# RWKV-7 recurrence: outputs made with features on partitions, products moved to the merges, and scores spread over the k stage

## The chip, the cores and the metric

The kernel runs on one core of one Trainium2 chip. The metric is the device time of one execution in microseconds (us); the median of three runs before the change is 2640.33 us (2639.37 to 2643.1). Five engines work beside each other, each in the order of its own program: TensorE (PE; its weight loads are PEld), VectorE (DVE), ScalarE (ACT), GpSimd (POOL) and SyncE (SP), which issues the DMAs.

## What is computed

A decoder trunk of two layers over 272 tokens (16 learned ones ahead of 256) with 2048 features: first an RWKV-7 time mix with an MLP behind it, then a gated linear attention with an MLP. The change touches only the time mix. Cut to what matters:

```python
r, k, v = xr @ w_rkv[0], xk @ w_rkv[1], xv @ w_rkv[2]      # 2048 x 2048 each
kk = kk / max(norm per head, 1e-12)                        # heads of 64 features
def step(S, inp):                                          # one token, S is 64 x 64 for each of 32 heads
    r_t, w_t, k_t, v_t, a_t, b_t = inp
    sa = einsum('bhvk,bhk->bhv', S, a_t)
    S = S * w_t + sa (x) b_t + v_t (x) k_t
    y = einsum('bhvk,bhk->bhv', S, r_t)
y = (y - mean) * rsqrt(var + eps) * ln_w + ln_b            # per head
out = ((y + bonus) * g) @ w_o                              # g: low-rank gate
```

The kernel doesn't run 272 steps. It takes chunks of 64 tokens, in which the recurrence becomes small matrix products and a triangular system.

## The kernel before, in words

Activations stand with features on partitions and tokens in the free dimension: 16 tiles of 128 features by 272 tokens. Every large product is split into two parts of float32: a weight tile of 128 x 1024 (`raw`) is rounded by ScalarE to `hi` (L134) and VectorE takes the rest, `lo` (L135); three products (L140 to L142) then make one 128 x 128 block of weights, which is called a unit below. `wload` puts these three steps ahead of other work by a priority; apart from the stretch named below a scheduler fixes the order on each engine by priorities and its own estimate of times.

**The k stage** is the loop over 16 output tiles f with L452. Each tile takes 16 units, then ScalarE and VectorE make decayed and normalised keys (`kk`, `kn`), with one product that sums over heads (L465) and one for the bonus (L480), and write the operands `bk` and `ar` to memory (`bkd`, `ard`). Output tiles lie in PSUM banks: `pj` (two) for even f, `pt` (two, from `ptr`) for odd f. For the recurrence, four groups g of eight heads (four feature tiles) are formed. In tile 3 the mixed input of the v projection is made, in tile 4 `load(0)` fetches the operands of group 0 (`BK`, `AR`), and in tile 6 all five calls of `scores(0, c)` follow each other: for each chunk eight products (L416) into two `pt` banks, and a mask by VectorE (L268, `AM`). From tile 8 on, seven steps per tile of `invert(0)` are added: VectorE inverts the triangular systems with transposes (L431, L434, L445, L449) and 30 pairs of small operations on `sysA`.

**The recurrence** comes after. In it the order on TensorE is the order of the code (`manual_schedule`); the other engines stay with the scheduler. `R(n)` runs n units of the products that wait to be done (the v projection, then the output product, in all 512 units), `until(n)` runs them up to the nth. For each group g and each of five chunks c (four of 64 tokens, one of 16) a step consists of `state` (L597, products with the state `sb`), `R(GAPS[g][c][0])`, `solve` (L607), `centre` (v minus its mean, every other chunk, L558), `carry` (L617, the old state times the identity into a new accumulator), `R(GAPS[g][c][1])`, `learn` (L623, the new state), `inner` for the next chunk (L579), `emit` (L632, the outputs, tokens on partitions, into the only bank `pry`) and `keys` (L569). ScalarE copies the output to `yc` (L635); one step later `turn` (L643) turns it by products with the identity to features on partitions, and ScalarE copies that to `hres` (L645). In between stand, for the next group, `scores(g + 1, c)` in the first two steps and the steps of `invert(g + 1)` from the end of step 1, nine at a time; for the last group, `norm` (L656 and L665 with what lies between them), two calls at a time in steps 2 and 3.

A group ends with `until(MARK[g])`, then `merge(g + 1)` joins the two halves of each inverse: one transpose (L526), a copy into `AMr` (L527), products L535, four copies, products L545, four copies. Then come `centre`, `keys` and `inner` of the new group's first chunk.

Of the kernel before, what the change touches and what calls it, by code (L numbers as in the profile page):

```python
# [45 lines left out]
GAPS = [[(2, 1), (2, 1), (8, 8), (9, 9), (9, 9)],  # L46
# [7 lines left out]
class Kern:  # L54
# [211 lines left out]
    def rwkv(self, done):  # L266
# [185 lines left out]
        for f in range(KT):  # L452
            r = rr[f]
            bk, ar = st2[0][f % 2], st2[1][f % 2]
            ps = self.proj(pair(wk, f), xk, T, bank=self.ptr if f % 2 else None)
# [27 lines left out]
            if f == 3:  # L483
                xv = mix(3, self.xp)
                early2.close()
                wl = ExitStack()
                lp = wl.enter_context(tc.tile_pool(name="wl", bufs=1, reuse_waits="tile"))
                BKs, ARs = ([self.t(lp, [P, 4, 576], n)] for n in ("BK0", "AR0"))
                AMs, AMrs = [self.t(lp, [P, NC4, 8, 128], "AM0")], [self.t(lp, [64, 8, 64], "AMr0")]
                sysA = self.t(lp, [P, 32, 32], "sysA")  # L490
                t11 = sysA.rearrange("p a b -> p (a b)")[64:96].rearrange("p (c h s) -> p c h s", c=NC4, h=8)
                nc.gpsimd.memset(sysA, 0.0)
            if f == 4:
                load(0)
# [17 lines left out]
        uvs, ras, bkts, rys, ys, pSs = {}, {}, {}, {}, {}, {}  # L512

        def geom(g, c):
            full = c < NC4
            n = C if full else 32
            lo, up = slice(0, n), slice(n, 2 * n)


            return full, n, C if full else T - NC4 * C, (AMs[g % 2][:, c] if full else AMrs[g % 2]), lo, up, ((lo, up), (up, lo))  # L520


        def merge(g):
# [3 lines left out]
            nc.scalar.copy(AMr[32:64, :, 0:16].rearrange("p h t -> p t h"), rg[:, :, 0:8])  # L527
# [46 lines left out]
        def inner(g, c):  # L574
            full, n, nr, am, lo, up, at = geom(g, c)
            uv = uvs[g, c]
            ra = ras[g, c] = half(self.pu())
            for h in range(8):
                nc.tensor.matmul(ra[at[h % 2][0], h // 2], am[:n, h, :n], uv[:n, h], start=h < 2, stop=c == 0 and h > 5)  # L579
            if c == 0:  # L580
                sides(g, c)

        def sides(g, c):
            full, n, nr, am, lo, up, at = geom(g, c)
            rs = ras[g, c, "rs"] = self.t(kp, [P, 512], "rs", 2).rearrange("p (h v) -> p h v", h=8)
            for q in range(2):
                nc.scalar.mul(rs[up, q::2], ras[g, c][at[q][0]], -1.0)


        def state(g, c):  # L590
# [3 lines left out]
            for p in range(4):  # L594
                for q, i in ((0, 0), (1, 1), (1, 0), (0, 1)):
                    rows = slice(64 * q, 64 * q + 64)
                    nc.tensor.matmul((ra, ry)[i][at[q][i], p], AR[rows, p, c * 128 + i * n : c * 128 + (i + 1) * n],  # L597
                                     sb[rows, p], start=i == 1 and p == 0, stop=i == 0 and p == 3)
# [14 lines left out]
        def carry(g, c):  # L613
            pS = pSs[g, c] = half(self.pu())
            if c:
                for p in range(4):
                    nc.tensor.matmul(pS[:, p], self.ident, sb[:, p], start=p == 0, stop=False)  # L617
# [9 lines left out]
        def emit(g, c):  # L627
# [7 lines left out]
            nc.scalar.copy(y[: 2 * n], ry[: 2 * n])  # L635

        def turn(g, c):
            full, n, nr = geom(g, c)[:3]
            y, py = ys[g, c], self.ptr()
            for p in range(4):  # L640
                for q in range(2):
                    rows = slice(n * (1 - q), n * (1 - q) + n)
                    nc.tensor.matmul(py[64 * q : 64 * q + 64, p * C : p * C + n], y[rows, p], self.ident[rows, rows],  # L643
                                     start=True, stop=True)
            nc.scalar.copy(hres[:, 4 * g : 4 * g + 4, c * C : c * C + nr],  # L645
                           py[:, : 4 * C].rearrange("p (f t) -> p f t", f=4)[:, :, :nr])

        def norm(g):
            for f in range(4 * g, 4 * g + 4):

                g2 = self.t(kp, [P, 2, P], "g2", 2)
                nc.sync.dma_start(g2, ap["g2"][f])
                sq = self.t(kp, [P, T], "ysq", 2)
                nc.scalar.activation(sq, hres[:, f], AF.Square)
# [3 lines left out]
                nc.scalar.activation(sq, sq, AF.Exp, scale=-0.5)  # L658
                yield
# [3 lines left out]
                pg = self.pm()[:, :T]  # L663
# [100 lines left out]
        with tc.manual_schedule(engines={mybir.EngineType.PE}):  # L764
# [4 lines left out]
            next(m)  # L769
            until(64)  # L770
            for f in (centre, keys, inner):
                f(0, 0)
            inv = last = nothing
            for g in range(NG):
                more = g + 1 < NG
                for c in range(5):
                    if c:
                        state(g, c)
                        turn(g, c - 1)
# [12 lines left out]
                    some(last, 2 if more and 1 < c < 4 else 0 if more else 4)  # L792
# [18 lines left out]
                if more:  # L811
# [11 lines left out]
                else:  # L823
                    turn(g, 4)
# [259 lines left out]
```

## Time and profile before

| | us |
|---|---|
| median of three runs | 2640.33 |
| profiled execution | 2640.85 |
| its span, first to last instruction | 2639.1 |
| k stage, first product of tile 0 to the first merge | about 165 to 332 |
| recurrence from the first merge to the last step | 332 to 640 |

The page of a profile gives busy times of each engine, the chain of work that ended last, and groups of instructions by line. Answers of the trace are shown in four forms. A row of a stage gives its bounds, its length, busy times of PE, PEld, DVE, ACT and POOL with counts, the granted TensorE clock (1 is full), and the share and rate of the DMA engines. A row of waits names who waited for whom: the sum in us, how often, and the longest. A row of the timeline has the start, the duration, the engine, the line and operation, what is written and read, and in brackets idle time ahead of it with what ended it. A product of two float32 operands stands twice in a count (x16 for eight products). Matmuls overlap, so what one costs is the distance from its start to the next start.

### The profile page before, as it was taken

How to read it: one execution, taken by the hardware profiler on the slowest of the kernel's cores; microseconds unless marked ns; L12 is line 12 of the kernel's file. 1: busy time of each engine (PE TensorE's matmuls, PEld its weight loads, DVE VectorE, ACT ScalarE, POOL GpSimd, SP SyncE). 2: the span in 40 equal slices, each digit the busy share in tenths (PEclk: the TensorE clock that was granted, in tenths of full speed). 3: DMA queues.
4: the chain of work that ended last, by engine and by line, in shares of the span. 5: the costliest groups of instructions: out<-in, count | busy, mean ns of one | idle time of the engine just before them, and what ended most of it. 6: DMA issues, size and time to landing. Idle time of an engine off the chain costs nothing.

```text
span 2639.1 us, 47851 instructions
## 1 busy us (share of the span) xinstructions
PE 2564.8 (97%) x19588; PEld 2373.6 (90%) x19588; DVE 1661.4 (63%) x2734; ACT 1271.9 (48%) x2075; POOL 10.8 (0%) x35
## 2 busy tenths in 40 slices
PE   7998998989999999999999999999999999999998
PEld 7887887878999999999999989998888888888887
DVE  8677966674755545545546666676766656656565
ACT  5364644455544434434434454454555535445444
POOL 0000000000000000000000000000000000000000
PEclk9998998999999999999999999999999999999999
DMA  5565742232455555545555544454555555555554
GB/s 195 175 216 204 242 148 81 96 103 93 162 176 176 176 176 176 176 176 176 176 176 176 182 147 151 145 176 144 189 186 188 187 190 186 191 185 190 188 188 160
DMA packets 137084, 450.18 MB, mean 171 GB/s; under 512 B 15760, under 2 KB 23696, under 8 KB 136864
## 3 DMA queue, kind: packets, MB, share of 16 engines
q1 hardware_dynamic: 136864, 447.12, 48.9%
q8 instruction: 153, 2.51, 0.4%
q14 instruction: 67, 0.55, 0.1%
HBM read 431.07 MB, written 15.99 MB: 169 GB/s over the span
## 4 chain that ended last, share of the span: by engine, by line
PE 90%; DVE 5%; ACT 2%; DMA 2%; issue 1%; SPq 0%; DVEq 0%; ACTq 0%
PE pj L168 23%; PE pj L140 15%; PE pj L142 15%; PE pj L141 15%; PE pj L169 12%; DVE lo L135 1%; PE pt L416 1%; PE pj L195 1%; ACT hi L134 1%; PE pt L919 1%; DVE sysA L431 0%; PE pm L665 0%; DVE upd L268 0%; PE pm L558 0%; DVE sysA L268 0%
## 5 line engine op out<-in xcount | busy, mean ns | idle before, releaser
L134 ACT CAST hi<-raw 128x1024 fp32r<-128x1024 f32 (+1 forms) x834 | 813.5, 983 | 1085.0 <-PE pj L141 565.0
L135 DVE TENSOR_TENSOR lo<-raw,hi 128x1024 fp32r<-128x1024 f32 (+1 forms) x834 | 946.9, 1142 | 607.1 <-ACT hi L134 598.2
L140 PE MATMUL pj<-x,hi 128*128 128x272 f32 x2224 | 657.3, 296 | 9.6 <-ACT x L308 4.3
L142 PE MATMUL pj<-x,lo 128*128 128x272 f32 x2224 | 646.3, 291 | 2.9 <-DVE lo L135 2.8
L141 PE MATMUL pj<-x,hi 128*128 128x272 f32 x2224 | 644.0, 290 | 0.0
L168 PE MATMUL pj<-x,hi 128*128 128x512 f32 x1664 | 587.1, 396 | 0.6 <-DVE x L838 0.6
L169 PE MATMUL pj<-x,lo 128*128 128x256 f32 x1664 | 467.4, 281 | 1.3 <-DVE lo L135 1.3
L140 PEld LDWEIGHTS pj<-x,hi 128*128 128x128 f32 x2224 | 421.6, 190 | 17.9 <-ACT x L308 5.0
L141 PEld LDWEIGHTS pj<-x,hi 128*128 128x128 f32 x2224 | 424.3, 191 | 2.1
L142 PEld LDWEIGHTS pj<-x,lo 128*128 128x128 f32 x2224 | 421.3, 189 | 4.7 <-DVE lo L135 3.7
L168 PEld LDWEIGHTS pj<-x,hi 128*128 128x128 f32 x1664 | 313.2, 188 | 76.9 <-issue 2.9
L168 PE MATMUL pj<-h,hi 128*128 128x512 f32 x1024 | 358.5, 394 | 0.0
L169 PEld LDWEIGHTS pj<-x,lo 128*128 128x128 f32 x1664 | 314.1, 189 | 2.3 <-DVE lo L135 1.9
L140 PE MATMUL pj<-h,hi 128*128 128x272 f32 x1024 | 294.7, 288 | 0.0
L142 PE MATMUL pj<-h,lo 128*128 128x272 f32 x1024 | 293.9, 287 | 0.0
L141 PE MATMUL pj<-h,hi 128*128 128x272 f32 x1024 | 293.6, 287 | 0.0
L169 PE MATMUL pj<-h,lo 128*128 128x256 f32 x1024 | 288.5, 282 | 0.0
L168 PEld LDWEIGHTS pj<-h,hi 128*128 128x128 f32 x1024 | 192.4, 188 | 44.5
L141 PEld LDWEIGHTS pj<-h,hi 128*128 128x128 f32 x1024 | 193.7, 189 | 0.0
L169 PEld LDWEIGHTS pj<-h,lo 128*128 128x128 f32 x1024 | 193.5, 189 | 0.0
L140 PEld LDWEIGHTS pj<-h,hi 128*128 128x128 f32 x1024 | 192.6, 188 | 0.0
L142 PEld LDWEIGHTS pj<-h,lo 128*128 128x128 f32 x1024 | 192.1, 188 | 0.0
(245 smaller groups left out, 2230.5 us busy)
## 6 DMA issues: line engine op xcount, KB each, us to landing
raw<-mlp_w_d SPq DMA_DIRECT2D x512, 512.0 KB, 3.2
raw<-gla_in_d SPq DMA_DIRECT2D x98, 512.0 KB, 3.2
raw<-w_rkv_d SPq DMA_DIRECT2D x80, 512.0 KB, 3.8
raw<-gla_o_d SPq DMA_DIRECT2D x32, 512.0 KB, 3.2
raw<-w_r_d SPq DMA_DIRECT2D x16, 512.0 KB, 3.3
raw<-rw_oA_d SPq DMA_DIRECT2D x16, 512.0 KB, 3.2
raw<-rw_oB_d SPq DMA_DIRECT2D x16, 512.0 KB, 3.2
ard<-ar SPq DMA_DIRECT2D x16, 288.0 KB, 4.1
```

The costliest lines, as they stand in the source:

```text
L134: nc.scalar.copy(hi[:, h], raw[:, h])
L135: nc.vector.tensor_tensor(out=lo[:, h], in0=raw[:, h], in1=hi[:, h].bitcast(F32), op=ALU.subtract)
L140: nc.tensor.matmul(out, hi[:, ws], xh, start=first, stop=False)
L141: nc.tensor.matmul(out, hi[:, ws], xl, start=False, stop=False)
L142: nc.tensor.matmul(out, lo[:, ws], xh, start=False, stop=last)
L168: nc.tensor.matmul(wide, hi[:, ws], x[kt][:, :, off : off + SEQ], start=kt == 0, stop=False)
L169: nc.tensor.matmul(ps[:, :SEQ], lo[:, ws], x[kt][:, 0, off : off + SEQ], start=False, stop=kt == nk - 1)
L195: nc.tensor.matmul(ps[:, :n], raw[:, j * P : (j + 1) * P], x(kt), start=kt == 0, stop=kt == 8 * len(srcs) - 1)
L416: nc.tensor.matmul(pv[q][:, p], BK[rows, p, cs], AR[rows, p, cs], start=True, stop=True)
L919: nc.tensor.matmul(pa[:w, i * C : (i + 1) * C], KX[i][:, dt, s * P : s * P + w], Q[:, dt, i * C : (i + 1) * C], start=dt == 0, stop=dt == 1)
```

## The change

In the recurrence `emit` and the output half of `state` change the roles of their operands: the state or `uv` is now the stationary one, and the output comes with features on partitions. It goes from `pry` straight to `hres` with one copy, so `turn`, `yc` and their copies are gone. `carry` is one product of 256 columns instead of four of 64. The `AMr` copy in `merge` goes from ScalarE to VectorE. `GAPS` gives the first two steps more units and the later ones fewer; at a merge six units stand between its halves as before (a `turn` no longer among them), three between it and `centre`, three between `centre` and `keys`. In `norm` the gate's product goes to a `pt` bank, the Square of the next tile is asked for one tile earlier, and three calls stand at a time. In the k stage the banks are `pj`, `pj`, `pry`; the v mix is made in tile 0, `load(0)` in tile 3, one score chunk in each of the tiles 5 to 9, and the inversion runs nine steps per tile from tile 10.

```diff
-GAPS = [[(2, 1), (2, 1), (8, 8), (9, 9), (9, 9)],
...
+GAPS = [[(4, 3), (4, 3), (8, 7), (8, 7), (6, 6)],
...
-            ps = self.proj(pair(wk, f), xk, T, bank=self.ptr if f % 2 else None)
+            ps = self.proj(pair(wk, f), xk, T, bank=self.pry if f % 3 == 2 else None)
...
-            if f == 3:
+            if f == 0:
                 xv = mix(3, self.xp)
...
-            if f == 4:
+            if f == 3:
                 load(0)
-            if f == 6:
-                for c in range(5):
-                    scores(0, c)
+            if 4 < f < 10:
+                scores(0, f - 5)
+            if f == 9:
                 inv = invert(0)
-            if f > 7:
-                for _ in range(7):
+            if f > 9:
+                for _ in range(9):
                     next(inv, None)
...
-            nc.scalar.copy(AMr[32:64, :, 0:16].rearrange("p h t -> p t h"), rg[:, :, 0:8])
+            nc.vector.tensor_copy(AMr[32:64, :, 0:16].rearrange("p h t -> p t h"), rg[:, :, 0:8])
...
-                    nc.tensor.matmul((ra, ry)[i][at[q][i], p], AR[rows, p, c * 128 + i * n : c * 128 + (i + 1) * n],
-                                     sb[rows, p], start=i == 1 and p == 0, stop=i == 0 and p == 3)
+                    if i:
+                        nc.tensor.matmul(ry[rows, p, :nr], sb[rows, p], AR[rows, p, c * 128 + n : c * 128 + n + nr],
+                                         start=p == 0, stop=False)
+                    else:
+                        nc.tensor.matmul(ra[at[q], p], AR[rows, p, c * 128 : c * 128 + n], sb[rows, p],
+                                         start=False, stop=p == 3)
...
-                for p in range(4):
-                    nc.tensor.matmul(pS[:, p], self.ident, sb[:, p], start=p == 0, stop=False)
+                nc.tensor.matmul(pS, self.ident, sb, start=True, stop=False)
...
-                nc.tensor.matmul(ry[at[h % 2][1], h // 2], am[: 2 * n, h, n : 2 * n], uv[: 2 * n, h],
+                k = slice(64 * (h % 2), 64 * (h % 2) + 64)
+                nc.tensor.matmul(ry[k, h // 2, :nr], uv[: 2 * n, h], am[: 2 * n, h, n : n + nr],
                                  start=c == 0 and h < 2, stop=h > 5)
-            y = ys[g, c] = self.t(kp, [P, 4, HEAD], "yc", 2)
-            nc.scalar.copy(y[: 2 * n], ry[: 2 * n])
-
-        def turn(g, c):
...
+            nc.scalar.copy(hres[:, 4 * g : 4 * g + 4, c * C : c * C + nr], ry[:, :, :nr])
...
+                if f < 4 * g + 3:
+                    nxt = square(f + 1)
                 yield
...
-                pg = self.pm()[:, :T]
+                pg = self.ptr()[:, :T]
...
+            R(2)
             until(64)
-            for f in (centre, keys, inner):
+            centre(0, 0)
+            R(3)
+            for f in (keys, inner):
                 f(0, 0)
+            R(4)
...
-                    some(last, 1 if not more else 2 if 1 < c < 4 else 0)
+                    some(last, 1 if not more else 3 if 1 < c < 4 else 0)
...
-                    some(last, 2 if more and 1 < c < 4 else 0 if more else 4)
+                    some(last, 3 if more and 1 < c < 4 else 0 if more else 4)
...
                     next(m)
-                    R(4)
-                    turn(g, 4)
-                    R(2)
+                    R(6)
                     next(m)
-                    for f in (centre, keys, inner):
+                    R(3)
+                    centre(g + 1, 0)
+                    R(3)
+                    for f in (keys, inner):
                         f(g + 1, 0)
                     R(4)
```

Three places of the programs show how instructions move. On TensorE at the end of the sixth tile of the k stage, before (`pj_2391` is tile 6, `pt_2546` tile 7, `pt_2486` and the like are the scores):

```order
L142 MATMUL pj_2391<-x_1151,lo_2425 128x272
L465 MATMUL pm_2463<-sq_2456,cst_117 128x272
L416 MATMUL pt_2486<-AR_433_2194,BK_432_2193 128x128
L416 MATMUL pt_2487<-AR_433_2194,BK_432_2193 128x128
...
L416 MATMUL pt_2534<-AR_433_2194,BK_432_2193 64x64 x4
L416 MATMUL pt_2535<-AR_433_2194,BK_432_2193 64x64 x4
L140 MATMUL pt_2546<-x_1136,hi_2549 128x272
```

The same place now (`pj_2510` is tile 7):

```order
L142 MATMUL pj_2510<-x_1140,lo_2514 128x272
L465 MATMUL pm_2475<-sq_2468,cst_117 128x272
L416 MATMUL pt_2391<-AR_391_1909,BK_390_1908 128x128
L416 MATMUL pt_2392<-AR_391_1909,BK_390_1908 128x128
...
L140 MATMUL pj_2510<-x_1141,hi_2513 128x272
...
L416 MATMUL pt_2498<-AR_391_1909,BK_390_1908 128x128 x3
L416 MATMUL pt_2499<-AR_391_1909,BK_390_1908 128x128 x3
...
L140 MATMUL pj_2510<-x_1143,hi_2513 128x272
```

The 40 score products stood in one block, with no product of a tile between them; the first two chunks now stand in tile 7 with two units between them, the other three follow at the ends of tiles.

On TensorE at the merge into group 1, before (L535 and L545 are the merge, L643 the last `turn`, L558 `centre`, L569 `keys`, L579 `inner`):

```order
L535 MATMUL pt_4772<-sysA_2197,AM_647_3521 32x32 x16
...
L643 MATMUL pt_4804<-cst_117,yc_4691 64x32 x8
...
L545 MATMUL pt_4847<-AM_647_3521,rs_4773 32x32 x16
L558 MATMUL pm_4866<-cst_117,hres_72 128x128 x4
L569 MATMUL pm_4875<-cst_117,BK_645_3519 128x128 x4
L579 MATMUL pu_4882<-uv_4871,AM_647_3521 64x64 x8
L140 MATMUL pj_4722<-x_2121,hi_4734 128x272
```

And now:

```order
L535 MATMUL pt_4718<-sysA_1912,AM_647_3521 32x32 x16
...
L545 MATMUL pt_4783<-AM_647_3521,rs_4719 32x32 x16
L140 MATMUL pj_4668<-x_1836,hi_4680 128x272
...
L558 MATMUL pm_4811<-cst_117,hres_72 128x128 x4
L140 MATMUL pj_4668<-x_1839,hi_4680 128x272
...
L569 MATMUL pm_4832<-cst_117,BK_645_3519 128x128 x4
L579 MATMUL pu_4839<-uv_4816,AM_647_3521 64x64 x8
```

Three units stand on either side of `centre`, and no `turn` between the halves.

On VectorE at the end of that inversion, before:

```order
L268 TENSOR_TENSOR r_13_87<-r_13_87,hres_72 128x272
L268 TENSOR_TENSOR upd_4522<-sysA_2197 128x30
L268 TENSOR_TENSOR sysA_2197<-sysA_2197,upd_4522 128x30
L445 STREAM_TRANSPOSE sysA_2197<-sysA_2197 32x8x32 x4
L449 STREAM_TRANSPOSE AM_647_3521<-sysA_2197 32x8x32
L135 TENSOR_TENSOR lo_4700<-raw_4697,hi_4699 128x512 x2
```

And now, with the transpose and the copy of `merge` that stand some twenty rows ahead:

```order
L526 STREAM_TRANSPOSE rs_4695<-sysA_1912 32x512
L268 TENSOR_TENSOR sysA_1912<-sysA_1912,upd_4455 128x9x22
L527 COPY AMr_648_3522<-rs_4695 32x16x8
...
L135 TENSOR_TENSOR lo_4681<-raw_4678,hi_4680 128x512 x2
...
L445 STREAM_TRANSPOSE sysA_1912<-sysA_1912 32x8x32 x4
L449 STREAM_TRANSPOSE AM_647_3521<-sysA_1912 32x8x32 x2
L135 TENSOR_TENSOR lo_4756<-raw_4753,hi_4755 128x512 x2
```

`lo_4700` was first used by TensorE ahead of L535, `lo_4681` is first used two units after it: VectorE now makes a weight that stands behind the merge's first product before it ends the inversion that this product needs.

More of the change, by code (lines that the diff above doesn't have):

```diff
@@ L511, in rwkv @@
         half = lambda x: x[:, :256].rearrange("p (h v) -> p h v", h=4)
-        uvs, ras, bkts, rys, ys, pSs = {}, {}, {}, {}, {}, {}
+        uvs, ras, bkts, rys, pSs = {}, {}, {}, {}, {}
         def geom(g, c):
@@ L517, in geom @@
             lo, up = slice(0, n), slice(n, 2 * n)
-            return full, n, C if full else T - NC4 * C, (AMs[g % 2][:, c] if full else AMrs[g % 2]), lo, up, ((lo, up), (up, lo))
+            return full, n, C if full else T - NC4 * C, (AMs[g % 2][:, c] if full else AMrs[g % 2]), lo, up, (up, lo)
         def merge(g):
@@ L578, in inner @@
             for h in range(8):
-                nc.tensor.matmul(ra[at[h % 2][0], h // 2], am[:n, h, :n], uv[:n, h], start=h < 2, stop=c == 0 and h > 5)
+                nc.tensor.matmul(ra[at[h % 2], h // 2], am[:n, h, :n], uv[:n, h], start=h < 2, stop=c == 0 and h > 5)
             if c == 0:
@@ L586, in sides @@
             for q in range(2):
-                nc.scalar.mul(rs[up, q::2], ras[g, c][at[q][0]], -1.0)
+                nc.scalar.mul(rs[up, q::2], ras[g, c][at[q]], -1.0)
         def state(g, c):
@@ L631, in emit, with square @@
             for h in range(8):
-                nc.tensor.matmul(ry[at[h % 2][1], h // 2], am[: 2 * n, h, n : 2 * n], uv[: 2 * n, h],
+                k = slice(64 * (h % 2), 64 * (h % 2) + 64)
+                nc.tensor.matmul(ry[k, h // 2, :nr], uv[: 2 * n, h], am[: 2 * n, h, n : n + nr],
                                  start=c == 0 and h < 2, stop=h > 5)
-            y = ys[g, c] = self.t(kp, [P, 4, HEAD], "yc", 2)
-            nc.scalar.copy(y[: 2 * n], ry[: 2 * n])
-        def turn(g, c):
[L638 to L646, printed above, removed]
-        def norm(g):
+            nc.scalar.copy(hres[:, 4 * g : 4 * g + 4, c * C : c * C + nr], ry[:, :, :nr])
+        def norm(g):
+            def square(f):
+                sq = self.t(kp, [P, T], "ysq", 2)
+                nc.scalar.activation(sq, hres[:, f], AF.Square)
+                return sq
+            nxt = square(4 * g)
+            yield
             for f in range(4 * g, 4 * g + 4):
+                sq = nxt
                 g2 = self.t(kp, [P, 2, P], "g2", 2)
                 nc.sync.dma_start(g2, ap["g2"][f])
-                sq = self.t(kp, [P, T], "ysq", 2)
-                nc.scalar.activation(sq, hres[:, f], AF.Square)
                 va = self.pm()[:, :T]
@@ L778, in rwkv @@
                         state(g, c)
-                        turn(g, c - 1)
                     if more and c < 2:
                         scores(g + 1, 2 * c)
-                    some(last, 1 if not more else 2 if 1 < c < 4 else 0)
+                    some(last, 1 if not more else 3 if 1 < c < 4 else 0)
                     R(GAPS[g][c][0])
@@ L815, in rwkv @@
                     next(m)
-                    R(4)
-                    turn(g, 4)
-                    R(2)
+                    R(6)
                     next(m)
-                    for f in (centre, keys, inner):
+                    R(3)
+                    centre(g + 1, 0)
+                    R(3)
+                    for f in (keys, inner):
                         f(g + 1, 0)
                     R(4)
-                else:
-                    turn(g, 4)
                 last = norm(g)
```

4 rows, old and new, of the table GAPS are left out of this document.

## The prediction

> **What bounds the kernel now.** I read the page first, then the stages around the change, then who waits, then single instructions. TensorE (PE) is the bound nearly everywhere, so a saving counts only where it shortens PE's own work or a wait of PE.
>
> ```profile
> PE 2564.8 (97%) x19588; PEld 2373.6 (90%) x19588; DVE 1661.4 (63%) x2734; ACT 1271.9 (48%) x2075; POOL 10.8 (0%) x35
> ```
>
> Next come the stages. The first row holds the score chunks of the k stage; the last four begin at the first product of a merge (L535).
>
> ```profile
> core 0: us, PE busy (x) PEld busy (x) DVE busy (x) ACT busy (x) POOL busy (x), PEclk, DMA share, GB/s
> 219.70:249.60 29.90, 23.52 (x148) 20.69 (x149) 19.07 (x49) 7.57 (x16) 0.16 (x1) 0.66 0.37 137
> 249.60:332.40 82.80, 77.97 (x565) 73.36 (x563) 78.68 (x220) 50.96 (x99) 0.00 (x0) 1.00 0.73 236
> 332.40:408.50 76.10, 70.46 (x1017) 63.65 (x1016) 53.53 (x120) 35.92 (x89) 1.63 (x3) 0.93 0.37 131
> 408.50:491.20 82.70, 76.24 (x1050) 66.81 (x1049) 56.54 (x131) 40.59 (x101) 1.62 (x3) 0.96 0.31 107
> 491.20:573.80 82.60, 74.48 (x1026) 64.67 (x1025) 57.92 (x138) 41.72 (x105) 1.62 (x3) 0.94 0.23 75
> 573.80:640.00 66.20, 61.62 (x930) 53.35 (x930) 22.24 (x44) 40.20 (x101) 0.52 (x1) 1.00 0.27 88
> ```
>
> Almost all that the diff touches lies in these rows; what comes after 640 I leave as it is. Two things stand out. In the first row the granted clock is 0.66 and DVE is busy for only 19 of 30 us. And in each of the four recurrence rows PE idles for 5 to 8 us, and in three of them it loses 4 to 7% of its clock. The waits that the change aims at:
>
> ```profile
> PE pm L665 <- ACT ysq L657: 6.4, 10, 0.9
> PE pm L569 <- ACT uv L564: 5.1, 4, 1.3
> PE pry L597 <- ACT yc L635: 2.1, 6, 0.9
> ```
>
> **Term A, the k stage.** Before, all five score chunks stand behind tile 6, whose head sums (L465) are the first row; the third is that product for tile 7, the fourth for tile 15, and the last two show one chunk alone and what follows it.
>
> ```profile
> 219.75 0.72 PE L465 MATMUL pm<-sq,cst 128*128 128x272 f32 x2 [1.86 <-ACT sq L462]
> 223.76 2.08 PE L416 MATMUL pt<-AR,BK 64*128 64x128 f32 x16 [3.29 <-DMA AR<-ard]
> ...
> 249.59 0.62 PE L465 MATMUL pm<-sq,cst 128*128 128x272 f32 x2
> ...
> 311.36 0.73 PE L465 MATMUL pm<-sq,cst 128*128 128x272 f32 x2
> ...
> 348.23 1.16 PE L416 MATMUL pt<-AR,BK 64*128 64x128 f32 x16
> 349.32 0.39 PE L140 MATMUL pj<-x,hi 128*128 128x272 f32 x1
> ```
>
> Tile 6 to tile 7 takes 249.59 - 219.75 = 29.8 us; the eight tiles after it take (311.36 - 249.59) / 8 = 7.7 us each. So 22.1 us go to the chunks, and five unhindered ones cost 5 x 1.09 = 5.5 us. PE could win 16.6 us when they stand one to a tile and their masks run under products. DVE doesn't allow all of it:
>
> ```profile
> 221.50:329.90 108.40, 98.26 (x688) 91.40 (x688) 95.97 (x265) 55.83 (x108) 0.16 (x1) 0.91 0.62 204
> ```
>
> Up to 329.9, where the first merge's transpose starts, DVE (the third busy column) works 95.97 of 108.4 us, and it has the same work afterwards, so at most 12.4 us go. I take 9: the load of AR moves on SP's queue ahead of tile 4's two writes but behind one more weight load, so one to two of its 3.29 us remain, and nine inversion steps per tile (seven before) crowd into six tiles instead of eight. Ends: 3.3 (that wait alone) and 12.4. Three banks for the tile outputs instead of four I cost at nothing: they cover three tiles, 23 us; if that cover were gone, the cost is a share of DVE's lag, which A's lower end holds. Moving the v mix from tile 3 to tile 0 shifts DVE's work by two or three rows; nothing.
>
> **Removed products.** A `turn` costs the stretch from its first product (L643) to the next block; the four identity products of `carry` (L617) are set against a product of the other layer with the same array size and 256 columns (L928).
>
> ```profile
> 352.85 0.64 PE L643 MATMUL pt<-cst,yc 64*64 64x64 f32 x16
> 353.42 0.48 PE L416 MATMUL pt<-AR,BK 64*128 64x128 f32 x2
> ...
> 359.14 1.10 PE L617 MATMUL pu<-S,cst 128*128 128x64 f32 x8
> ...
> 1539.85 0.70 PE L928 MATMUL pu<-A,V 128*128 128x256 f32 x2
> ```
>
> That is 0.57 us for each of 20 turns, and 1.10 - 0.70 = 0.4 us for each of 12 carries. The products of `state` and `emit` keep their number and array size: nothing. The 20 yc copies taken off ScalarE lie beside other work.
>
> **Term B, the three spans from merge to merge.** PE would win much here, but the inversion on DVE decides how much. It starts with L431, and L445 must end before the next merge's first product.
>
> ```profile
> 360.56 0.61 DVE L431 STREAM_TRANSPOSE sysA<-AM 32x256 f32<-32x256 f32 x1
> 401.16 2.14 DVE L445 STREAM_TRANSPOSE sysA<-sysA 32x256 f32<-32x256 f32 x4
> 437.26 1.11 DVE L431 STREAM_TRANSPOSE sysA<-AM 32x256 f32<-32x256 f32 x2
> 479.16 2.18 DVE L445 STREAM_TRANSPOSE sysA<-sysA 32x256 f32<-32x256 f32 x4
> 517.88 1.61 DVE L431 STREAM_TRANSPOSE sysA<-AM 32x256 f32<-32x256 f32 x3
> 566.17 2.28 DVE L445 STREAM_TRANSPOSE sysA<-sysA 32x256 f32<-32x256 f32 x4
> ```
>
> ```profile
> 362.00:404.00 42.00, 38.89 (x533) 35.38 (x532) 39.68 (x98) 20.70 (x52) 0.68 (x2) 0.94 0.38 133
> 483.24 0.40 ACT L527 COPY AMr<-rs 32x128 f32<-32x128 f32 x1 [6.26 <-DVE rs L526]
> ```
>
> The chain takes 42.7, 44.1 and 50.6 us, with DVE busy 39.68 of 42. Before, the merges follow its end by 5.2, 9.9 and 5.3 us (408.5, 491.2 and 573.8 less those ends). Part of that is the L527 copy: ScalarE sat 6.26 us in it with weight casts queued behind. On DVE it costs 0.4 us and blocks nobody. But the chain now starts after more products. From merge to L431 it was 28.2, 28.8 and 26.7 us. To it come 15, 14 and 14 units, since the first two steps have 14 instead of 6 and the merge has more.
>
> ```profile
> 395.73 0.29 PE L142 MATMUL pj<-x,lo 128*128 128x272 f32 x1
> 396.10 0.29 PE L142 MATMUL pj<-x,lo 128*128 128x272 f32 x1
> 399.77 0.59 PE L142 MATMUL pj<-x,lo 128*128 128x272 f32 x1 [2.14 <-DVE lo L135]
> 402.59 0.43 PE L142 MATMUL pj<-x,lo 128*128 128x272 f32 x1
> 405.31 0.43 PE L142 MATMUL pj<-x,lo 128*128 128x272 f32 x1
> ```
>
> A unit costs 0.37 us (395.73 to 396.10), so 5.6, 5.2 and 5.2 us come on top. Away go one turn or two and a carry (0.9, 1.5, 1.5) and the merge's wait for uv (1.3 each), which three units now cover; without that cover it comes back. With the first two merges a half-clock stretch goes too: after 399.77 a unit takes 2.72 / 4 = 0.68 us (402.59 to 405.31), so about 6.8 us at that pace cost 3.1. The starts come out at 28.5, 28.1 and 29.1. PE has some 15 units (5.6 us) less between start and merge, so it will stand at the merges waiting for DVE, which is late next; I add 3 us of half clock to the second and third start: 31.1 and 32.1. Within the chain stood 14, 10 and 10 half conversions of weights, now 12 each, so I take 41.4, 45.4 and 50.6 us, the last with idle DVE time of its own to hold it. The new spans are 69.9, 76.5 and 82.7, in all 229.1 for 241.4: B = 12. Ends: 0, if no stall goes and each merge adds half clock, and 43, which is PE's idle of 5.6 + 6.5 + 8.1 us, its lost clock of 5.3 + 3.3 + 5.0 and the removed products of 9.
>
> On the clock, the Trainium skill (TensorE: Matmul & The Clock Gate, "What's actually happening") says that half speed comes after an idle window of about 3.4 us. Here a wait of 2.14 us was followed by it, so the trace is stricter than the rule. By the rule the new waits at merges cost only themselves when they come in pieces under 3.4 us.
>
> **Term C, the last group**, 573.8 to 640, has no inversion: PE decides. Idle of 4.6 us, six turns (3.4) and three carries (1.2) make 9.2 at most; at least the products, 4.6. Much of the idle is L665 waiting for ScalarE in the bank it shares with L656, which the new bank ends. The Square, asked for one tile earlier, now stands behind Ln and Exp of the tile before, so one product in a group may wait anew, by no more than 0.9 (L665's longest). I take 7.
>
> **Sum.** 9 + 12 + 7 = 28 us off the profiled execution's 2640.85 us, which is 0.5 us over the median of the runs: 2612 us.
>
> **Rivals.**
> - PE sets the pace of the merges, because DVE, never starved, runs the chain faster than its rows show. With half of B's far end (22), A 12 and C 9 the gain is 43: 2598 us. For it: PE's vanishing waits are plain rows. Against it: 39.68 of 42 us busy.
> - Waits at merges in short pieces, with no half clock behind them: the two 3 us in B stay away, 2606 us. Against it: the half clock after 2.14 us. This is what the Trainium skill's rule above would make of them.
> - The inversion eats the gain: B 0, A 4, C 5, so 2632 us. For it: fewer units beside the chain and a later start.
> - No change, 2640 us: the products removed only lengthen waits for DVE, and the k stage's waits on masks turn into waits on the bonus products.
> - Slower: the output sums now leave the single pry bank by one strided copy into hres, and `state` of the next step writes that bank right after `emit` and `keys`. Before, L597 waited 2.1 us in six cases for yc. Were the copy to come behind weight casts in all 16 steps, the change turns to a loss from 28 / 16 = 1.75 us a step on; at 2.2 us it is 2647 us. Against it: the longest of those waits was 0.9.
>
> **Chances.** DVE-paced merges as summed 0.42; PE-paced 0.18; no half clock 0.08; chain eats the gain 0.22; no change 0.06; slower 0.04. A measurement of this kernel tells 0.2% (5.3 us) from no change. Faster 0.42 + 0.18 + 0.08 + 0.22 = 0.90, same 0.06, slower 0.04. The range leaves out the last two and the outer part of the PE-paced case: 2592 to 2632.
>
> **What would show it.** Right: L416 in the k stage without waits on masks, tile 15's L465 some 9 us earlier; no L643; the merges' first products waiting for DVE; the AMr copy on DVE; L569 without its wait; half-clock stretches only near merges. Wrong: DVE idle between L431 and L445 (then PE paces), `state` waiting for hres, or a k stage in which the bonus products (L480) wait in sum as long as the scores did.

## The result, and the profile after

The kernel after takes 2621.17 us, the median of five runs (2618.45 to 2625.59); the kernel before took 2640.33 (2632.56 to 2649.08) beside it. The ratio is 0.9927 with an interval of 0.9906 to 0.9949: 19 us, where 28 were forecast. The profiled execution took 2618.45 us, 22.4 less than the profiled one of before. The page's row of busy times, and the stages with the bounds moved to the same instructions (the first row is tile 6 to tile 7 of the k stage, the last four begin at the first product of a merge, L535):

```profile
PE 2552.0 (98%) x19196; PEld 2364.0 (90%) x19196; DVE 1660.6 (63%) x2738; ACT 1263.7 (48%) x2051; POOL 10.8 (0%) x35
```

```profile
217.80:230.90 13.10, 11.27 (x100) 9.96 (x99) 8.74 (x21) 6.12 (x12) 0.00 (x0) 1.00 0.82 300
230.90:317.70 86.80, 80.86 (x594) 75.38 (x595) 84.13 (x240) 51.71 (x101) 0.16 (x1) 1.00 0.67 224
317.70:394.70 77.00, 70.01 (x933) 62.73 (x934) 56.98 (x129) 34.59 (x85) 1.63 (x3) 0.93 0.40 140
394.70:471.50 76.80, 73.81 (x950) 65.52 (x950) 56.30 (x131) 38.48 (x95) 1.62 (x3) 0.94 0.32 108
471.50:551.20 79.70, 69.97 (x929) 61.04 (x929) 58.75 (x140) 40.15 (x99) 1.63 (x3) 0.95 0.25 86
551.20:620.00 68.80, 67.56 (x826) 59.44 (x827) 23.04 (x46) 37.29 (x92) 0.52 (x1) 0.86 0.24 77
```

The k stage's row fell from 29.9 to 13.1 us at full clock, with three of the five score chunks left in it. The three spans fell by 8 us in all. The last row is the surprise: PE is busy for 67.56 of 68.80 us, yet at a clock of 0.86. An instruction that both kernels share behind all this work, the first product of the next norm (L225), dates its end, here in the kernel before and after:

```profile
714.25 0.73 PE L225 MATMUL pm<-acc,cst 128*128 128x272 f32 x2
```

```profile
693.29 0.50 PE L225 MATMUL pm<-acc,cst 128*128 128x272 f32 x1
```

The way from the fourth merge to it took 714.25 - 573.8 = 140.5 us before and 693.29 - 551.17 = 142.1 after. So the sum of these two profiles reads: first merge 14.7 us earlier (332.38 to 317.71), spans 8.0, last group -1.7, the rest 1.4, in all 22.4. A second profile of the kernel after (below, "The kernel after once more") has 692.00 - 554.10 = 137.9 us between these two marks, so this one part differs by 4.2 us between executions of one program.

In the k stage of after, on TensorE's timeline, three chunks stand between the head sums of tiles 6 and 7, and the wait for AR is 1.43. The other two chunks stand one to a tile, and one wait for a mask is left (0.58 us at 237.56, where before there were four of 2.5 us in all):

```profile
217.83 0.73 PE L465 MATMUL pm<-sq,cst 128*128 128x272 f32 x2
219.99 1.16 PE L416 MATMUL pt<-AR,BK 64*128 64x128 f32 x16 [1.43 <-DMA AR<-ard]
...
222.03 1.62 PE L416 MATMUL pt<-AR,BK 64*128 64x128 f32 x16
...
227.16 1.16 PE L416 MATMUL pt<-AR,BK 64*128 64x128 f32 x16
...
230.91 0.73 PE L465 MATMUL pm<-sq,cst 128*128 128x272 f32 x2 [0.41 <-ACT sq L462]
...
295.38 0.50 PE L465 MATMUL pm<-sq,cst 128*128 128x272 f32 x1
```

The last row is tile 15's L465, 16.0 us earlier than before, of which 2.6 lie ahead of the k stage's loop (tile 0's L465 came at 174.12 for 176.68). The three waits that the change aims at have become these (L654 is the head sum of the norm; L665, which waited in ten places, no longer waits):

```profile
PE pm L569 <- ACT uv L564: 3.6, 3, 1.2
PE pm L654 <- ACT ysq L655: 2.5, 2, 1.6
PE pry L598 <- ACT hres L638: 1.3, 4, 0.6
```

The chains on VectorE (L431 to L445) for the second to fourth merge, and the merges' first products on TensorE:

```profile
351.83 0.61 DVE L431 STREAM_TRANSPOSE sysA<-AM 32x256 f32<-32x256 f32 x1
392.48 2.08 DVE L445 STREAM_TRANSPOSE sysA<-sysA 32x256 f32<-32x256 f32 x4
425.28 0.62 DVE L431 STREAM_TRANSPOSE sysA<-AM 32x256 f32<-32x256 f32 x1
467.87 2.24 DVE L445 STREAM_TRANSPOSE sysA<-sysA 32x256 f32<-32x256 f32 x4
498.48 0.61 DVE L431 STREAM_TRANSPOSE sysA<-AM 32x256 f32<-32x256 f32 x1
548.95 2.08 DVE L445 STREAM_TRANSPOSE sysA<-sysA 32x256 f32<-32x256 f32 x4
```

```profile
317.71 0.38 PE L535 MATMUL pt<-sysA,AM 32*32 32x32 f32 x13 [1.47 <-DVE sysA L445]
394.70 0.34 PE L535 MATMUL pt<-sysA,AM 32*32 32x32 f32 x5 [4.28 <-DVE sysA L445]
471.51 0.38 PE L535 MATMUL pt<-sysA,AM 32*32 32x32 f32 x12
551.17 0.33 PE L535 MATMUL pt<-sysA,AM 32*32 32x32 f32 x5 [5.42 <-DVE sysA L445]
```

Chains take 42.7, 44.8 and 52.5 us, and each merge follows its chain's end by 0.1 to 1.4 us, where before it was 5.2, 9.9 and 5.3. VectorE now paces the second and the fourth, at which PE waits 4.28 and 5.42 us; the third stands 1.4 us behind its chain, and PE doesn't wait there.

What went wrong shows on TensorE's timeline in `state` of the 16-token chunk (c = 4), here the first group's in the kernel after, with the block that follows:

```profile
376.13 0.30 PE L601 MATMUL pu<-S,AR 64*32 64x64 f32 x2
376.68 0.28 PE L598 MATMUL pry<-AR,S 64*64 64x16 f32 x2 [0.25 <-ACT hres L638]
376.89 0.30 PE L601 MATMUL pu<-S,AR 64*32 64x64 f32 x2
377.12 0.28 PE L598 MATMUL pry<-AR,S 64*64 64x16 f32 x2
...
379.76 0.28 PE L598 MATMUL pry<-AR,S 64*64 64x16 f32 x2
379.98 0.59 PE L140 MATMUL pj<-x,hi 128*128 128x272 f32 x1
```

Before, all sixteen products of this block used 32 columns of the array, and in the fourth group it took 1.1 us, from 627.23 to 628.34:

```profile
627.23 0.30 PE L597 MATMUL pu<-S,AR 64*32 64x64 f32 x2
...
628.34 0.68 PE L643 MATMUL pt<-cst,yc 64*64 64x64 f32 x16
```

Now products of 32 and of 64 columns alternate, one after another every 0.22 us: 379.98 - 376.13 = 3.85 us. The chunks of 64 tokens give the comparison within one kernel: their sixteen products go to the same two outputs in the same alternating order, but all with 64 columns, and take 0.62 us (344.19 to 344.82). So neither the two outputs nor the changed roles cost the time. In the fourth group the block ends at 606.47, and this stretch, without any wait of PE, runs at half clock:

```profile
605.30:619.00 13.70, 13.70 (x82) 12.32 (x82) 3.43 (x6) 5.22 (x13) 0.00 (x0) 0.50 0.13 41
```

### The profile page after: what moved, and what is told of

Its sections match the earlier page's. It is cut to its first block, busy times and chain, and to the rows that moved or that the text cites. A ratio compares the mean times of both kernels' runs of the same rounds, so it can differ in the third digit from the quotient of the medians.

```text
span 2616.7 us, 47047 instructions
## 1 busy us (share of the span) xinstructions
PE 2552.0 (98%) x19196; PEld 2364.0 (90%) x19196; DVE 1660.6 (63%) x2738; ACT 1263.7 (48%) x2051; POOL 10.8 (0%) x35
## 4 chain that ended last, share of the span: by engine, by line
PE 81%; DVE 3%; ACT 1%; issue 0%; DVEq 0%
PE pj L168 24%; PE pj L140 13%; PE pj L142 13%; PE pj L141 13%; PE pj L169 12%; DVE lo L135 1%; PE pt L921 1%; PE pu L930 0%; PE pt L665 0%; PE pt L416 0%; DVE upd L268 0%; DVE sysA L431 0%; DVE sysA L268 0%; PE pu L611 0%; PE pm L558 0%; PE pu L601 0%
## 5 line engine op out<-in xcount | busy, mean ns | idle before, releaser
L140 PE MATMUL pj<-x,hi 128*128 128x272 f32 x2272 | 677.3, 298 | 7.5 <-ACT x L308 4.2
L142 PE MATMUL pj<-x,lo 128*128 128x272 f32 x2272 | 662.3, 292 | 0.0
L141 PE MATMUL pj<-x,hi 128*128 128x272 f32 x2272 | 661.5, 291 | 0.5 <-DVE x L268 0.5
L140 PEld LDWEIGHTS pj<-x,hi 128*128 128x128 f32 x2272 | 434.2, 191 | 16.3 <-ACT x L308 4.9
L141 PEld LDWEIGHTS pj<-x,hi 128*128 128x128 f32 x2272 | 436.9, 192 | 3.0 <-DVE x L268 0.7
L142 PEld LDWEIGHTS pj<-x,lo 128*128 128x128 f32 x2272 | 433.8, 191 | 1.1 <-DVE lo L135 0.3
L168 PEld LDWEIGHTS pj<-x,hi 128*128 128x128 f32 x1664 | 312.4, 188 | 76.6 <-issue 2.9
L169 PEld LDWEIGHTS pj<-x,lo 128*128 128x128 f32 x1664 | 313.3, 188 | 2.3 <-DVE lo L135 1.9
L168 PEld LDWEIGHTS pj<-h,hi 128*128 128x128 f32 x1024 | 192.4, 188 | 44.4
```

The source lines that it names most:

```text
L140: nc.tensor.matmul(out, hi[:, ws], xh, start=first, stop=False)
L141: nc.tensor.matmul(out, hi[:, ws], xl, start=False, stop=False)
L142: nc.tensor.matmul(out, lo[:, ws], xh, start=False, stop=last)
L168: nc.tensor.matmul(wide, hi[:, ws], x[kt][:, :, off : off + SEQ], start=kt == 0, stop=False)
L169: nc.tensor.matmul(ps[:, :SEQ], lo[:, ws], x[kt][:, 0, off : off + SEQ], start=False, stop=kt == nk - 1)
```

## The experiments

The theory: the block's two widths are what the prediction missed, VectorE's chain paces the merges, and the k stage's gain is its own. "The reordered kernel" is the first experiment's. Executions of one kernel differ by up to 0.9% (before: 2633.39 to 2655.66 beside the first four), so a few us are read from marks in the profiles, of which each run has one.

**The widths.** Edit to the kernel after:

```diff
+            seq = [(p, q, i) for p in range(4) for q, i in ((0, 0), (1, 1), (1, 0), (0, 1))]
+            if not full:
+                seq.sort(key=lambda x: x[2])
```

> The kernel after, with the sixteen state products of the 16-token chunk in another order: first the eight with a 32-wide stationary operand (for the triangular right-hand side), then the eight with a 64-wide one (for the output). Theory W (products of two tile widths that alternate follow each other at 0.22 us each, and the stretch brings half clock): the block takes at most 1.4 us instead of 3.7 to 4.7, the 13.7 us of half clock behind the fourth group's block go, and the last group ends 8 to 10 us earlier; in the first three groups part of the 2.5 us each turns into waiting for VectorE at the merges. In all 9 us (5 to 18) off the kernel after: 28 us off the kernel before, ratio about 0.989. Rival M (a moving operand of 16 columns makes each output product slow, whatever stands beside it): the block stays above 2.2 us, 2 to 4 us off. Rival C (the half clock behind it is not the block's doing): the block is short, the half clock stays, 2.5 to 5 us off.

2613.68 us, ratio 0.9878 (0.9849 to 0.9908). Its timeline on TensorE, and the next norm's mark:

```profile
375.13 0.64 PE L603 MATMUL pu<-S,AR 64*32 64x64 f32 x16
375.70 0.64 PE L600 MATMUL pry<-AR,S 64*64 64x16 f32 x16
376.27 0.39 PE L140 MATMUL pj<-x,hi 128*128 128x272 f32 x1
```

```profile
681.64 0.50 PE L225 MATMUL pm<-acc,cst 128*128 128x272 f32 x1
```

The same products take 1.14 us. All four half-clock stretches behind the blocks are gone, and 681.64 - 548.46 = 133.2 us from the fourth merge to the mark are 8.9 less than in the profile of after above, and 4.7 less than in its second one. In the three spans only 3.2 us came: there PE stands longer for VectorE (L535 waits 19.4 us in four places, for 11.2 in three). This is theory W; rivals M and C fall.

The dose, an edit to the reordered kernel:

```diff
-                seq.sort(key=lambda x: x[2])
+                seq.sort(key=lambda x: (x[0] // 2, x[2]))
```

> The reordered kernel, with the sixteen state products of the 16-token chunk in four runs of four of one width instead of two runs of eight: three changes of width instead of one (and fifteen in the kernel after). Theory W (each change of width costs, since the products on both sides of it don't overlap): by the two blocks measured, (3.84 - 1.14) / 14 = 0.19 us per change, so the block takes 1.14 + 2 x 0.19 = 1.5 us. Rival N (what costs is a mixed block as such, or short products that stand apart): 2.5 us or more. Rival O (only neighbours in pairs matter): 1.2 us or less.

```profile
378.56 0.41 PE L603 MATMUL pu<-S,AR 64*32 64x64 f32 x8
379.10 0.41 PE L600 MATMUL pry<-AR,S 64*64 64x16 f32 x8
379.44 0.41 PE L603 MATMUL pu<-S,AR 64*32 64x64 f32 x8
379.78 0.41 PE L600 MATMUL pry<-AR,S 64*64 64x16 f32 x8
380.12 0.39 PE L140 MATMUL pj<-x,hi 128*128 128x272 f32 x1
```

380.12 - 378.56 = 1.56 us, where 1.5 was worked out (2608.04 us in its one run). The cost goes by the changes of width, so rivals N and O fall. The Trainium skill (TensorEngine Tiling (Array Packing), "Key Properties") says that changing the tiling mode, not just the tile, drains the engine; the trace agrees, at some 0.2 us for each change here.

**The k stage alone**, in the kernel before:

```diff
+            ps = self.proj(pair(wk, f), xk, T, bank=self.pry if f % 3 == 2 else None)
...
+            if f == 0:
+                xv = mix(3, self.xp)
...
+            if f == 3:
+                load(0)
+            if 4 < f < 10:
+                scores(0, f - 5)
+            if f == 9:
                 inv = invert(0)
+            if f > 9:
+                for _ in range(9):
```

> The kernel before with the k stage's edits alone (banks, v mix in tile 0, load in tile 3, one score chunk per tile, nine inversion steps from tile 10). Theory K (what PE won in the k stage in the kernel after is a gain of these edits and reaches the end): first merge 14 to 15 us earlier, 15 us off the kernel before, ratio 0.9943. The prediction's term: 9 us, ratio 0.9966, if the merge stands behind VectorE's transpose and the AMr copy as before. Rival: the gain is waited away in the recurrence: under 5 us.

**All but the k stage**, the kernel after with these lines as they were before:

> The kernel after with the k stage of the kernel before: the recurrence's edits alone. If the terms add up as the two profiles show them (spans between merges 7.9 us less, last group 1.6 us more, 1 to 2 us less behind it): 5 to 8 us off the kernel before, ratio 0.9975. Prediction's terms: 19 us, ratio 0.993. Rival (the parts depend on each other: the AMr copy on VectorE is what lets the first merge start early): 10 us or more off here, and under 12 us with the k stage's edits alone.

The k stage alone: 2633.85 us, ratio 0.9963 (0.9942 to 0.9984). The rest alone: 2628.68 us, 0.9947 (0.9925 to 0.997). The sizes add up to more than the whole, and the intervals are wide: the first, 4 to 15 us, holds every expectation; the second, 8 to 20, holds the prediction's 19 and the rival's 10 or more, and the theory's 5 to 8 only at its edge. The rival's reason falls all the same, since in the k stage alone the first merge comes early with the AMr copy on ScalarE. The marks tell more. TensorE's program ahead of the first merge is the same in the k stage alone as in the kernel after, and yet the merge came at 324.64 and not 317.71: 7.7 us earlier than before, not the theory's 14 to 15. Half of what is missing is the start: tile 0's L465 lies anywhere from 174.0 to 178.7 us in the profiles, and here at 177.78. The other half is two stretches of half clock of 3.4 us each, behind waits of 1.97 us for AR and 1.61 us for a mask, an estimated 3.4 us lost; no other profile with these edits has half clock there. From tile 0's L465 to the first merge it is 155.7 and 155.5 us in the two profiles without the k stage's edits, and 142.7 to 146.9, on average 144.0, in the twelve with them (this one is the 146.9). So that part is worth 11.6 us, and 2.6 of the 14.7 above lie ahead of the change.

Then some of it is given back. From the first merge to the first L431, in the k stage alone and in the rest alone:

```profile
324.60:359.10 34.50, 30.46 (x422) 27.05 (x422) 13.31 (x24) 14.16 (x34) 0.94 (x1) 0.80 0.34 122
```

```profile
334.00:363.30 29.30, 28.31 (x444) 25.58 (x444) 11.75 (x20) 15.95 (x37) 0.95 (x1) 1.00 0.48 166
```

Where the first merge comes early, PE stands there 1.5 us for VectorE and 1.3 for ScalarE, and the clock falls to 0.80 over this stretch; the chain starts 5 us later after its merge. The kernel after has 34.1 us here, like the first. Of the three spans' sum, 241.4 us before and 233.5 after, the k stage's edits alone make 247.6 and the rest alone 231.7: by these profiles the recurrence's edits are worth 10 to 14, and the k stage takes 2 to 6 back.

**VectorE's chain.** The reordered kernel with half of the inversion's pairs left out for groups 1 to 3:

```diff
-            for s in range(1, 31):
+            for s in range(1, 16 if g else 31):
```

> The reordered kernel (state products of the 16-token chunk grouped by width), and the inversion of groups 1 to 3 leaves out its pairs 16 to 30 (later groups' results are changed by it). It takes some 12 to 15 us off each VectorE chain. Theory D (VectorE's inversion paces the second to fourth merge): the waits of the merges' first products for L445 (11 us in the kernel after) go with the half clock behind two of them; 10 to 15 us less than the reordered kernel with the full inversion. Rival P (PE paces the merges; the waits only show slack that something else would take): under 3 us less.

2587.24 us, ratio 0.9778 (0.9748 to 0.9808), 26 us less than the reordered kernel. On VectorE and TensorE the third merge now reads:

```profile
444.42 1.13 DVE L445 STREAM_TRANSPOSE sysA<-sysA 32x256 f32<-32x256 f32 x2
```

```profile
461.71 0.38 PE L535 MATMUL pt<-sysA,AM 32*32 32x32 f32 x12
```

The chain's end is 16 us ahead and no merge but the first waits; the spans are 69.4, 71.1 and 69.5 us, in all 20 less than the reordered kernel's 230.3, and no half clock stands from 333 to 2589 us. This is theory D, with more to win than I expected, since half clock goes at all three merges.

**An earlier start by fewer units**, an edit to the reordered kernel:

```diff
-GAPS = [[(4, 3), (4, 3), (8, 7), (8, 7), (6, 6)],
+GAPS = [[(2, 1), (2, 1), (8, 7), (8, 7), (6, 6)],      # and likewise in the next two rows
```

> The reordered kernel (state products of the 16-token chunk grouped by width) with fewer units in the first two steps of each of the first three groups (3 each, as in the kernel before, where the change has 7, 7 and 5); they are run instead at the group's end, ahead of the merge. Theory D (VectorE's chain paces the merges, so what matters is how soon it starts): each chain starts 1.5 to 3 us earlier, merges 2 to 4 together 5 to 9 us earlier, 5 to 9 us less than the reordered kernel. Rival S (the units cover waits of the steps, which come back): no gain; new waits of the state and solve products for ScalarE of 1 us a step. Rival P (only the sum of PE's work counts): no change.

2615.04 us, ratio 0.9905 (0.9881 to 0.9928): no gain. Chains start 0.6 to 2.5 us earlier (31.8, 30.2 and 26.0 us after their merges for 32.7, 30.8 and 28.5), and two of three are longer (44.4 and 46.5 for 42.7 and 46.2); the spans' sum is 229.8 for 230.3. No new wait of the state or solve products shows, so rival S isn't what the trace shows either. What took the units' place is half clock: over the three stretches from a merge to its L431 the granted clock is 0.89, 0.83 and 0.99, where the reordered kernel has 0.95, 0.90 and 0.94. By length times lost clock that is an estimated 2 us more in each of the first two stretches and 1.4 less in the third, against the 3, 3 and 1.5 us of the units taken out.

**An earlier start by the scores**, an edit to the reordered kernel (chunks 3 and 4 then stand in the first step, and the inversion is asked for there, seven steps at a time; the second step gets six units more; the first merge likewise):

```diff
-                    R(3)
+                    head(g + 2, 0, 3)              # scores(g + 2, 0), or R(3) where no group is left
                     centre(g + 1, 0)
-                    R(3)
+                    head(g + 2, 1, 3)
...
-                    R(4)
+                    head(g + 2, 2, 4)
```

> The reordered kernel, with the next group's score chunks moved from the first two steps to the merge (three) and the first step (two), in the place of ten units that are run at the group's end; the inversion starts one step earlier and is asked for seven steps at a time. Theory D: chains start 10 to 13 us sooner after each merge, the merges no longer wait for VectorE, spans fall to PE's pace of 69 to 71 us (sum about 210 for 230), no half clock after the first merge: 18 to 25 us less than the reordered kernel, about 45 to 50 us off the kernel before, ratio 0.982. Rival L (VectorE's work and the weights' low halves share the engine, so an earlier start lengthens the chain by as much): under 6 us less. Rival A (scores at the merge wait for the operands' loads or for the banks they share with the merge): new waits of L416 of 2 to 3 us at each merge, 8 to 14 us less.

2596.2 us, ratio 0.9835 (0.9813 to 0.9858); once more, in other rounds:

> The kernel with the score chunks at the merges and two buffers for ysq once more, for comparison in the same rounds: 46 us off the kernel before, ratio 0.9835.

2597.77 us, 0.9838 (0.9822 to 0.9854). The first of the chains on VectorE, and the merge behind it:

```profile
344.80 0.62 DVE L431 STREAM_TRANSPOSE sysA<-AM 32x256 f32<-32x256 f32 x1
383.39 2.18 DVE L445 STREAM_TRANSPOSE sysA<-sysA 32x256 f32<-32x256 f32 x4
```

```profile
393.67 0.32 PE L535 MATMUL pt<-sysA,AM 32*32 32x32 f32 x8
```

Chains start 9 to 15 us sooner, merges 2 to 4 don't wait, the spans are 72.2, 73.7 and 72.8 us. How much less than the reordered kernel it is depends on the measure: 11 us by the ratios, 12 and 15 by the marks from tile 0's L465 to L225, 16 and 17 by the medians of different rounds. That is rival A's 8 to 14 or a little more, and short of theory D's 18 to 25. In the second profile L416 waits 4.4 us for loads and masks from the first merge on, and the norm's head sum waits 6.2 us, where in the reordered kernel it was 2.5.

**The kernel after once more**, in the same rounds:

> The kernel after once more, so that the variants can be compared with it in the same rounds: 0.9927 of the kernel before, 19 us off; merges at VectorE's pace (the first product of each within 0.2 to 1.5 us of the inversion's last transpose).

2621.76 us, 0.9929 (0.9908 to 0.9951). In this profile the merges follow the chains' ends by 0.15, 1.25 and 0.15 us, and the spans' sum is 232.3 us. The fourth group's block is followed by 3.4 us of half clock, where it was 13.7 in the first profile. At half speed that is an estimated 5.1 us less lost, and the way from the fourth merge to L225 takes 137.9 us for 142.1.

**The AMr copy**, in the reordered kernel:

```diff
-            nc.vector.tensor_copy(AMr[32:64, :, 0:16].rearrange("p h t -> p t h"), rg[:, :, 0:8])
+            nc.scalar.copy(AMr[32:64, :, 0:16].rearrange("p h t -> p t h"), rg[:, :, 0:8])
```

> The reordered kernel with the AMr copy of the merge on ScalarE as in the kernel before. The prediction held that this copy, 6.26 us on ScalarE at the second merge, was part of what kept the merges behind the chain's end. If so, spans grow by 2 to 5 us each and the kernel by 5 to 12 us. My reading now (the copy is read by the last chunk's products alone, a whole group later, and the merges stand within 0.1 us of the chain's end): no change within 3 us.

2611.36 us, 0.9887 (0.9866 to 0.9908): the same as with it on VectorE, as expected.

**The norm's wait**, in the kernel with the scores at the merges:

```diff
-                sq = self.t(kp, [P, T], "ysq", 2)
+                sq = self.t(kp, [P, T], "ysq", 3)      # and, in a second kernel, 4
```

> The kernel with the score chunks at the merges and the grouped state products, and three buffers for ysq instead of two. The prediction put a new wait of the norm's head sum on Ln and Exp ahead of the Square. Theory B (the Square waits for a buffer that VectorE still reads behind the inversion): ScalarE's wait for r at the Square (3 us and more each in steps 2) and PE's waits for ysq (6.2 us in two places, 3.5 the longest) shrink to under 1 us each, the half clock behind them (3.4 us at 437 and at 512) goes, 5 to 9 us less than with two buffers. Rival E (Ln and Exp ahead of it): the waits stay, no change within 2 us.

2597.41 us, 0.9846 (0.9829 to 0.9864), no change. ScalarE still stands, in front of the fourth tile's Square (with two buffers it was the third's):

```profile
432.08 0.43 ACT L646 ACTIVATE ysq<-hres 128x272 f32<-128x272 f32 x1 [5.33 <-DVE r L268]
```

> The kernel with the score chunks at the merges and four buffers for ysq, one for each tile of a group. With three, ScalarE's order has the fourth tile's Square, whose buffer VectorE still reads, ahead of the second and third tile's Ln and Exp, so the wait only moved. Theory B (the buffer that VectorE still reads is the cause): with four ScalarE no longer waits 5.3 us for r at the Square, PE's waits for ysq (6.2 us in two places) fall under 1.5 us, the half clock at 435 to 439 and 510 to 514 goes, 5 to 9 us less than with two buffers (2596 to 2598). Rival E (Ln and Exp ahead of it): the waits stay, no change within 2 us.

2591.93 us, 0.9835 (0.981 to 0.9859; one of six runs took 2609). By the ratios it can't be told from two buffers; by the profiles it is 6.9 us shorter from first to last instruction (2589.9 for 2596.8), 4.9 of it in the three spans between merges (214.6 for 219.5). ScalarE waits at no Square any more, but one of PE's two waits is left:

```profile
PE pm L656 <- ACT ysq L657: 3.5, 1, 3.5
```

```profile
503.47 0.42 ACT L677 CAST x<-hres 128x272 fp32r<-128x272 f32 x1 [4.36 <-DVE hres L668]
```

Ahead of the Ln and Exp there now stands another instruction that waits for VectorE. So theory B holds in kind, not in number: not Ln and Exp, but whatever in ScalarE's order needs a result of VectorE while that is in the inversion. This kernel, 46 us off the one before, has the shortest profile of those that compute the whole inversion.

## Why the prediction was off by 9 us

The direction held, and 2621 lies within 2592 to 2632; by its steps:

- **The failed step** is "The products of `state` and `emit` keep their number and array size: nothing." For c = 4 the output half of `state` went from 32 columns to 64 while the other half kept 32. That cost 2.7 us or more in each of four groups and brought half clock behind each. Grouped, with nothing else changed, the kernel is 29 us off the one before, where the sum had 28. That the two agree so well is partly luck, since errors within term B offset each other.
- **Term C** (7): it came out at -1.7 in one profile of the kernel after and at 140.5 - 137.9 = 2.6 in the other, and is 140.5 - 133.2 = 7.3 with the products grouped. The sum holds, its parts less well: a carry went from 0.91 us to 0.35, a gain of 0.56 where 0.4 was taken, and L665's waits in this group, now gone, were 1.2 us of the 4.6 of idle time and so not much of it. No run tests these parts one by one.
- **Term A** (9, ends 3.3 and 12.4): 11.6. The upper end was drawn at the start of the merge's transpose L526 (329.9 us before), as if the merge's first product needed it. It doesn't. On VectorE stand the chain's end L445 in the kernel before, and then L526 in the kernel after:

```profile
317.39 0.64 DVE L445 STREAM_TRANSPOSE sysA<-sysA 32x256 f32<-32x256 f32 x1
```

```profile
323.90 0.70 DVE L526 STREAM_TRANSPOSE rs<-sysA 32x512 f32<-32x512 f32 x1
```

  L526 came only 6 us earlier, now behind the merge's first product at 317.71. What that product needs is L445, which had ended 14.3 us ahead of the merge before. One to two us of the AR wait were to stay; 1.43 did.
- **Term B** (12): 8.0, and 241.4 - 230.3 = 11.1 with the products grouped. The chains are within 2 us of their forecast (41.4, 45.4, 50.6 against 42.7, 44.8, 52.5), and PE does stand at two of the three merges. The first chain was put too short by a count: 12 half conversions of weights stand in it before and after, not 14. The starts were 34.1, 30.6 and 27.0 for 28.5, 31.1 and 32.1. Half clock was added to the second and third start but not to the first, where A itself puts a wait; without A the first start is 29.3. The third was put too late twice: only 10 units come to it, since its first two steps have 10 and not 14, which takes 1.5 us off, and the third merge doesn't wait, so the 3 us of half clock are not there. So the first span came out 7 us longer than forecast and the third 3 us shorter. The cover of the wait for uv by three units failed: L569 still waits 3.6 us in three places; three chunks in their place leave 1.2 in one.
- **The AMr copy** was no part of what held the merges: back on ScalarE it changes nothing (2611.36 us for 2613.68), so ScalarE's 6.26 us in it lay beside other work.
- **The Square** was to make one product a group, the head sum behind it, wait anew by no more than 0.9. That product waits 2.5 us in two places, for another reason than the one named.
- **Rivals.** PE-paced merges fall with the chain's experiment. (The far end of that rival has a slip: by the prediction's own prices 14 turns and 9 carries make 11.6 us in the three spans, not 9, which moves its 2598 us by some 1 us.) The inversion doesn't eat the gain: its chains, 42.7, 44.8 and 52.5 us for 42.7, 44.1 and 50.6, are at most 2 us longer. The slower case did not come: the waits of `state` for hres are 1.3 us in four places, 0.6 the longest. No half clock falls: it stands behind merges that waited. By the Trainium skill's rule (TensorE: Matmul & The Clock Gate, "What's actually happening") an idle window of some 3.4 us is needed; the trace is stricter, with 1.5 and 1.3 us at the first merge, and at the fourth group's block of two widths half clock comes with no idle time in the rows.

## What to carry to other kernels

When operands change roles, compare the array's tile of each product with those that stand beside it in the order, for the odd-sized last chunk too: products of unequal widths want to stand in runs. When one engine's chain paces another, look for what lets the chain start sooner before making the other engine's work smaller. Draw an engine's limit at the instruction that the next stage waits for, not at the last one of the stage.

## What the runs showed of the hardware

- A change between products of 32 and of 64 columns costs some 0.2 us (fifteen changes 3.85 us, three 1.56, one 1.14). Eight equal ones in a run take 0.57 us, 0.07 us each, and sixteen of 64 columns that alternate between two outputs 0.62 us.
- Half clock doesn't need idle time: sparse products that follow each other at 0.22 us were followed by 3.4 to 13.7 us of it, the same block of the same kernel by 13.7 in one profile and 3.4 in another; the same products in 1.14 us by none.
- TensorE's same program from tile 0's L465 to the first merge took 142.7 to 144.9 us in eleven profiles at a full granted clock, and 146.9 in the one with 6.8 us of half clock.
- From the mark L225 to the end the profiles have 1923.3 to 1924.8 us, but two (half of the pairs left out; fewer units) have 1934.6, though no edit touches that part. The difference grows evenly over the first 770 us, dense products at a granted clock of 1.00 in all of them (769.3 us became 780.7). What makes it stays open. By its size it can explain why the profiled execution of each of these two is the longest of its runs (2598.62 of 2584.36 to 2598.62 us, 2623.12 of 2609.25 to 2623.12).
